# Output phase of a hybrid decoder layer: sums on VectorE over two blocks, norm weights applied in two steps

## The chip, the cores and the metric

The kernel runs on one core of a Trainium2 chip. A core has a matmul engine (TensorE, PE), VectorE (DVE), ScalarE (ACT), GpSimd (POOL) and SyncE (SP), which here only issues transfers between the main memory and the on-chip memory SBUF. Matmul results land in PSUM, eight banks of 512 float32 numbers for each of 128 partitions. The engines run side by side, each works its own queue in order, and they wait for each other by semaphores. The metric is the time of one execution in device microseconds (us), the median over several runs.

## The reference

One layer of a decoder is computed for 2048 new tokens of a prompt and for 32 sample tokens (8 sequences of 4). The width is 1024. Only the end of the layer matters here:

```python
pc = y_c @ w_out_c                              # short-convolution branch
pr = y_r @ w_out_r                              # RWKV branch
m = sigmoid(gc) * pc + sigmoid(gr) * pr         # gated merge
x = x + m @ w_o                                 # output projection and residual
y = x * rsqrt(mean(x * x, axis=-1) + 1e-6) * final_g      # last norm, a row is one token
```

All is float32. The inputs `y_c`, `y_r` and the gates come from a long first phase (projections, a convolution and the RWKV recurrence), which the change does not touch.

## The kernel before

**Products.** Each of the three projections is done for the tokens in two sets (d = 0 and 1) of 1024 rows; the sample tokens ride with set 1. A set's projection is cut into 2 x 2 quarters and computed by Strassen's scheme (in Winograd's form) with seven products of half size instead of eight. The operands of the products are sums of quarters. The sums of the weights were computed earlier and lie in main memory; those of the moving side are made here, by `make` (line 1865). To keep float32 accuracy, each operand is split into a high part (rounded by a ScalarE copy) and a low part (the rest, by a VectorE subtraction), and a product takes three matmuls: high by high, high by low, low by high.

**Stages.** `STAGES` (line 1657) orders the output phase: "r" for set 0 (RWKV branch), "o" for set 0 (output projection), "c" and "r" for set 1, "o" for set 1, seven products each, numbered through by `seq` (line 1863). Before them come some blocks of the "c" projection of set 0 (line 2062). In "c" and "r" (`merge_phase`, line 1934) the result lies with channels on the partitions. In "o" (`out_phase`, line 2001) it lies with tokens on the partitions, so that a row's norm can be taken. All products work in four blocks j of 128 partitions, and each block has its PSUM tile `acc[j]`. In "c" and "r" a block's twelve kt-by-part matmuls run one block after the other. In "o" a product takes its weights in two halves i; for each half the four blocks come in turn with six matmuls each.

**Emptying the banks.** After a block of "c" or "r", `merge_out` (line 1911) copies or adds the partial product to an SBUF quarter of M or R (called x1, x2, y1, y2), multiplies by the gate and, for "r", adds the quarter R to M (line 1930): on VectorE for x2, on POOL for the other three. After a block of "o", `out_done` (line 1964) adds the partial product to the residual rows, which were loaded into R's place. When half of a row is complete, `square` sums its squares on ScalarE. The first halves of rows (x1, y1) are complete in the products k = 1 and 4, the second halves in k = 5 and 6. Then `finish` (line 1956) adds both sums of squares, computes the reciprocal root with `rsq` (a power on POOL and a refining step in four small VectorE operations), multiplies both halves by it and by `final_g`, each with one VectorE operation over 512 columns, and stores them.

**Operands ahead.** `make(n + 2, j)` prepares the operand of the product after next into one of three rooms (UA, XH, XL) in turn, one block of 512 columns per instruction. The sums for "o" are x1 - x2 and y2 - (x1 - x2) for product k = 2 (VectorE; summed during k = 0, split during k = 1), x2 + y2 for k = 5 and y1 - y2 + (x1 - x2) for k = 6 (POOL, lines 1899, 1901, 1902).

**Samples.** Their 32 rows run as small extra matmuls (`out_samples`, line 1986) beside products of "o" in set 1: first halves in k = 0 and 1; second halves in the last product, which for this takes the weights "12" ahead of its own "22" (line 1662 orders the weights, line 2012 uses them).

**Order.** The weights stream through four buffers of 1 MB in the order of the list `order`; `take_w` issues loads up to three ahead, on SP's queue. Gates, operand quarters and residual rows go through the same queue at places fixed by `HOOKS` (line 2042). In this phase the program's text sets which operation depends on which; the order within each engine's queue is settled when the program is compiled, and ready work may come earlier than the text has it. All instructions pass through one recording helper, so the profile puts nearly all of them on line 264; tiles tell them apart.

Of the kernel before, what the change touches and what calls it, by code (L numbers as in the profile page):

```python
# [16 lines left out]
P = 128  # L17
# [327 lines left out]
def hybrid_kernel(tc, x_prompt, x_sample, state_conv, state_shift, state_rwkv, norm_g, w_in, conv_w,  # L345
# [1519 lines left out]
    def make(n, j, parts=(0, 1)):  # L1865

        if n >= len(seq):
            return
        w, d, k = seq[n]
        room = ROOMS[n % 3]  # L1870
        wd = NT if w == "o" else HW[d]
        src = Y if w != "o" else M

        def at(q):
            return src[q][:, j, 0:wd]

        def op(dst, a, b, o, eng):
            if 0 in parts:
                eng.tensor_tensor(out=dst, in0=a, in1=b, op=o)
        add, sub = ALU.add, ALU.subtract  # L1880
        if w != "o":
            t = at({0: "11", 2: "12", 3: "12", 4: "21", 5: "11", 6: "22"}.get(k, "11"))
            if k == 1:
                op(at("11"), at("12"), at("11"), sub, V)
                t = o2.tile([P, WQ], F32, name="st")[:, 0:wd]
                op(t, at("22"), at("11"), sub, V)
            if k == 2:
                op(t, at("22"), t, sub, V)
            if k == 3:
                op(t, at("22"), at("11"), sub, V)  # L1890
                op(t, at("21"), t, sub, V)
        else:
            t = at({0: "y1", 1: "x1", 3: "x1", 4: "y2", 5: "x2", 6: "y1"}.get(k, "x1"))
            if k == 2:
                op(at("x1"), at("x1"), at("x2"), sub, V)
                t = Y["21"][:, j, 0:wd]
                op(t, at("y2"), at("x1"), sub, V)
# [13 lines left out]
    def merge_out(w, d, k, j):  # L1911

        ps = acc[j][:, k == 4, 0:NT] if d == 0 else acc[j][:, :, 0:WQ // 2]

        def view(t):
            return t[:, 0:NT] if d == 0 else t.rearrange("p (a n) -> p a n", a=2)
        Q = M if w == "c" else R
        q = ("x1", "x2", "y2", "y1", "x1", "y2", "x2")[k]
        dst = view(Q[q][:, j, :])
        if k < 3:  # L1920
            A.copy(dst, ps)
            return
        g = gate_for(w, d, q, j)
        if k == 3:
            gate_mul(dst, ps, view(g))
        else:
            V.tensor_tensor(out=dst, in0=dst, in1=ps, op=ALU.add)
            gate_mul(dst, dst, view(g))
        if w == "r":
            (V if q == "x2" else G).tensor_tensor(out=M[q][:, j, 0:HW[d]], in0=M[q][:, j, 0:HW[d]], in1=R[q][:, j, 0:HW[d]], op=ALU.add)  # L1930
        if used[0] > 1:
            fetch_gate()

    def merge_phase(n):
        w, d, k = seq[n]
        room = ROOMS[n % 3]
        for j in range(NP):
# [12 lines left out]
            make(n + 2, j)  # L1950
# [4 lines left out]

    def finish(r, pieces, m=P):
        f = nwt.tile([P, 1], F32, name="fin", bufs=2)
        V.tensor_tensor(out=f, in0=fs[:, 0, r:r + 1], in1=fs[:, 1, r:r + 1], op=ALU.add)
        rsq(f, [P, 1], 1.0 / D, RMS_EPS)
        for half, (t, dst) in enumerate(pieces):  # L1960
            V.scalar_tensor_tensor(out=t, in0=t, scalar=f[0:m], in1=fg[0:m, half * 4 * P:(half + 1) * 4 * P], op0=ALU.mult, op1=ALU.mult)
            SP.store(dst, t)

    def out_done(d, k, j):
# [4 lines left out]
        if k in (1, 4, 5, 6):  # L1969
            r, half = rows_at(q, j)  # L1970
            square(o, r, half)
            if k > 4:
                finish(r, [(o_at(d, x, j), x_rows(d, x, j, y_prompt)) for x in (q[0] + "1", q[0] + "2")])
# [12 lines left out]
    def out_samples(half, base, wt, i, start, stop):  # L1986
# [6 lines left out]
    def samples_done(half):  # L1993
# [4 lines left out]
        if half:  # L1998
            finish(2 * NP, [(OS[0:NSAMP, i], y_sample.rearrange("j i d -> (j i) d")[:, i * 4 * P:(i + 1) * 4 * P]) for i in range(2)], NSAMP)

    def out_phase(n):
        w, d, k = seq[n]
        key = PRODUCTS["o"][k]
        if k == 0:
            V.memset(fs, 0.5 * D)
# [6 lines left out]
        if n == len(seq) - 1:  # L2012
            for i in range(2):
                out_samples(1, 0, take_w((w, d, "12", i)), i, i == 0, False)
            wts = [take_w((w, d, key, i)) for i in range(2)]
            for i in range(2):
                out_samples(1, NP, wts[i], i, False, i == 1)
# [6 lines left out]
        for i in range(2):  # L2024
            wt = take_w((w, d, key, i))
            for j in range(NP):
# [5 lines left out]
                if j % 2:  # L2032
                    c = 2 * i + j // 2
                    if k == 1:
                        make(n + 1, c, (1,))
                    make(n + 2, c, (0,) if k == 0 else (0, 1))
            if d and k < 2:
                out_samples(0, NP * (k == 0), wt, i, k + i == 0, k + i == 2)
        if d and k == 1:
            samples_done(0)  # L2040

# [20 lines left out]
    for i, b in enumerate(REST):  # L2062
# [13 lines left out]
        if i > 0:  # L2076
            make(0, i - 1)
    for j in range(NP):
        make(1, j)
# [35 lines left out]
```

## Time and profile before

| | |
|---|---|
| Median of three runs | 3118.93 us (3116.41 to 3121.59) |
| Profiled execution, its own time | 3117.36 us |
| Its span, first to last instruction | 3115.7 us |
| PE busy | 3017.7 us, 97% of the span |
| DVE busy | 2157.3 us, 69% |
| ACT busy | 1339.5 us, 43% |
| POOL busy | 389.5 us, 13% |
| Mean granted PE clock | 0.991 |
| Output phase, from its first matmul to the end of the span | 2648.6 to 3115.7 us |

A row of the order of time reads: start, duration, engine, operation, output from input with shapes, how many were merged into the row; in brackets how long the engine had been idle and who ended the wait. In the groups the last numbers before the bar are the total busy time and the mean of one in nanoseconds. The tile names are the kernel's, shortened: `Rx` and `Ry` are quarters of R, `Mx` and `My` of M, `acc` the PSUM tiles, `whl` the weights, `gt` the gates, `fin` and `nw` small tiles of the norm, `US` the sample operand, `OS` the sample rows.

### The profile page before, as it was taken

Reading aid. Unit: us, or ns where it says so; the run is one execution under the profiler, and the core shown is the slowest. Engines: PE = TensorE matmul, PEld = TensorE weight load, DVE = VectorE, ACT = ScalarE, POOL = GpSimd, SP = SyncE. Lnnn points to the kernel's source line nnn. Section 1 sums busy time; section 2 is a strip of 40 time slices with the busy share of each in tenths; the row PEclk is TensorE's granted clock in tenths of the full one; section 3 lists DMA queues with packets and bytes.
Section 4 is the critical chain, followed back from the end, with each engine's and each line's share of the span. In section 5 each row is a group of like instructions: output and inputs, shape, how many; then the busy total and the mean of one; then the engine's idle time right before and its main releaser. Section 6 shows DMA issues by size and latency. Waiting matters only on the chain. (4 is left out here: it accounts for less than half of the span.)

```text
span 3115.7 us, 56464 instructions
## 1 busy us (share of the span) xinstructions
PE 3017.7 (97%) x21418; PEld 2583.1 (83%) x21418; DVE 2157.3 (69%) x5713; ACT 1339.5 (43%) x2744; POOL 389.5 (13%) x568
## 2 busy tenths in 40 slices
PE   7899999999999999999999999999999999999998
PEld 6678777788778788788888889999999999779986
DVE  5577777766777777777766666766676773477675
ACT  4455555544444444444444344444444431323222
POOL 2011111111111110111111111000000000030040
PEclk9999999999999999999999999999999999999999
DMA  8687777756666676667644444444334448988765
GB/s 274 231 260 232 228 221 228 231 208 229 234 226 234 227 241 214 234 233 242 220 160 162 167 156 143 136 147 147 130 137 135 141 155 287 344 294 295 261 232 189
DMA packets 293941, 659.19 MB, mean 212 GB/s; under 512 B 46394, under 2 KB 162227, under 8 KB 242982
## 3 DMA queue, kind: packets, MB, share of 16 engines
q1 hardware_dynamic: 293670, 655.58, 62.3%
q8 instruction: 169, 2.77, 0.4%
q14 instruction: 102, 0.84, 0.1%
HBM read 472.81 MB, written 182.69 MB: 210 GB/s over the span
## 5 line engine op out<-in xcount | busy, mean ns | idle before, releaser
L264 PE MATMUL ip<-XH,whl 128*128 128x512 f32 (+3 forms) x7088 | 1944.9, 354 | 22.9 <-DVE whl L264 10.5
L264 PEld LDWEIGHTS ip<-XH,whl 128*128 128x128 f32 x7088 | 1225.9, 190 | 168.4 <-DVE whl L264 13.2
L264 PE MATMUL ip<-XL,whl 128*128 128x512 f32 (+3 forms) x3544 | 1250.4, 353 | 0.8 <-POOL XL L264 0.8
L264 PEld LDWEIGHTS ip<-XL,whl 128*128 128x128 f32 x3544 | 672.9, 190 | 71.5 <-issue 5.6
L264 DVE TENSOR_TENSOR tt<-Mi,X 128x60 f32<-128x60 f32 (+24 forms) x992 | 214.8, 217 | 28.9
L264 DVE TENSOR_TENSOR X<-X,tt 128x60 f32<-128x60 f32 (+24 forms) x992 | 211.7, 213 | 32.1
L264 DVE SCALAR_TENSOR_TENSOR S<-pb,pe,sp 64x64 f32<-64x64 f32 x512 | 143.3, 280 | 123.9 <-PE pb L264 116.9
L264 ACT ACTIVATE sp<-S,pe 128x128 f32<-128x128 f32 x256 | 102.5, 401 | 240.8 <-DVE S L264 237.5
L264 ACT COPY SV<-pb 64x128 f32<-64x128 f32 x256 | 66.1, 258 | 314.4 <-PE pb L264 312.0
L264 ACT ACTIVATE tmp<-ip,vec 128x512 f32<-128x512 f32 (+2 forms) x174 | 102.9, 593 | 206.8 <-PE ip L264 202.3
L264 DVE TENSOR_TENSOR UB<-pa,P 64x64 f32<-64x64 f32 x512 | 110.2, 215 | 117.3 <-PE pa L264 99.9
L264 DVE TENSOR_TENSOR whl<-wraw,whl 128x1024 fp32r<-128x1024 f32 x81 | 102.3, 1264 | 24.8 <-ACT whl L264 24.0
L264 ACT COPY Xbd<-Mi 32x256 f32<-32x256 f32 x128 | 88.2, 689 | 68.4 <-DVE Mi L264 66.1
L264 PEld LDWEIGHTS pb<-UB,Xbd 128*128 128x128 f32 x512 | 86.5, 189 | 33.9 <-PE ip L264 11.7
L264 ACT ACTIVATE tmp<-ip 128x512 f32<-128x512 f32 (+2 forms) x126 | 63.0, 500 | 117.9 <-PE ip L264 117.5
L264 DVE TENSOR_TENSOR GM<-pt,mask_p 128x512 f32<-128x512 f32 x128 | 82.6, 686 | 43.7 <-PE pt L264 43.4
L264 PEld LDWEIGHTS pa<-S,AR 128*128 128x128 f32 x512 | 88.9, 189 | 27.3 <-DVE S L264 14.9
L264 POOL COPY carry<-tmp 128x1 f32<-128x1 f32 x99 | 22.3, 225 | 708.2 <-ACT tmp L264 708.2
L264 PE MATMUL pb<-UB,Xbd 128*128 128x128 f32 x512 | 104.3, 285 | 3.9 <-DVE UB L264 3.1
L264 PEld LDWEIGHTS pb<-SV,BKt 128*128 128x128 f32 x512 | 89.8, 189 | 20.4 <-ACT SV L264 6.1
L264 PE MATMUL pa<-S,AR 128*128 128x128 f32 x512 | 102.1, 281 | 4.7 <-DVE S L264 4.5
L264 PE MATMUL pb<-SV,BKt 128*128 128x128 f32 x512 | 100.7, 278 | 1.4 <-ACT SV L264 1.4
(550 smaller groups left out, 4517.6 us busy)
## 6 DMA issues: line engine op xcount, KB each, us to landing
wraw<-in_w_in_dram SPq DMA_DIRECT2D x81, 512.0 KB
whl<-w_k SPq DMA_DIRECT2D x24, 1024.0 KB
whl<-w_r SPq DMA_DIRECT2D x24, 1024.0 KB
whl<-w_v SPq DMA_DIRECT2D x24, 1024.0 KB
whl<-w_z SPq DMA_DIRECT2D x24, 1024.0 KB
whl<-w_xin SPq DMA_DIRECT2D x24, 1024.0 KB
whl<-w_cg SPq DMA_DIRECT2D x24, 1024.0 KB
whl<-w_zc SPq DMA_DIRECT2D x24, 1024.0 KB
```

The source lines that it names most:

```text
L264: r = f(*a, **k)
```

## The change

All sums of the output phase go to VectorE: the additions of R to M, and the operands of the output products k = 5 and 6. `make` works on two blocks at a time, so its sums, copies and splits cover 2 x 512 columns (2 x 528 in set 1). The first half of a row is multiplied by `final_g` as soon as it is complete (`half_done`); `finish` then scales it by the row's factor with one ScalarE operation, and the second half as before with one VectorE operation. The sum of squares is scaled on the way, and the refining step gets shorter: its factor of -1/2 is put into `final_g` once. The samples' "12" weights and matmuls move from the last product to the end of product k = 1.

```diff
-            for k in ("12", "22") if (w, d, n) == ("o", 1, 6) else (k,):
+            for k in ("11", "12") if (w, d, n) == ("o", 1, 1) else (k,):
...
-    def make(n, j, parts=(0, 1)):
+    def make(n, c, parts=(0, 1)):
...
+        src, js = Y if w != "o" else M, slice(2 * c, 2 * c + 2)
+        hi, lo = (ROOMS[n % 3][:, i, js, 0:wd] for i in range(2))
...
             if k == 5:
-                op(t, t, at("y2"), add, G)
+                op(t, t, at("y2"), add)
             if k == 6:
-                op(t, t, at("y2"), sub, G)
-                op(t, t, at("x1"), add, G)
-        if 1 not in parts:
-            return
-        A.copy(room[:, 0, j, 0:wd], t)
-        V.tensor_tensor(out=room[:, 1, j, 0:wd], in0=t, in1=room[:, 0, j, 0:wd].bitcast(F32), op=sub)
+                op(t, t, at("y2"), sub)
+                op(t, t, at("x1"), add)
+        if 1 in parts:
+            A.copy(hi, t)
+            V.tensor_tensor(out=lo, in0=t, in1=hi.bitcast(F32), op=sub)
...
         if w == "r":
-            (V if q == "x2" else G).tensor_tensor(out=M[q][:, j, 0:HW[d]], in0=M[q][:, j, 0:HW[d]], in1=R[q][:, j, 0:HW[d]], op=ALU.add)
+            V.tensor_tensor(out=M[q][:, j, 0:HW[d]], in0=M[q][:, j, 0:HW[d]], in1=R[q][:, j, 0:HW[d]], op=ALU.add)
...
-            make(n + 2, j)
+            if j % 2:
+                make(n + 2, j // 2)
...
+    def half_done(t, r, m=P):
+
+        V.tensor_scalar(out=fs[0:m, 0, r:r + 1], in0=fs[0:m, 0, r:r + 1], scalar1=1.0 / D, scalar2=RMS_EPS, op0=ALU.mult, op1=ALU.add)
+        V.tensor_tensor(out=t, in0=t, in1=fg[0:m, 0:4 * P], op=ALU.mult)
+
     def finish(r, pieces, m=P):
-        f = nwt.tile([P, 1], F32, name="fin", bufs=2)
-        V.tensor_tensor(out=f, in0=fs[:, 0, r:r + 1], in1=fs[:, 1, r:r + 1], op=ALU.add)
-        rsq(f, [P, 1], 1.0 / D, RMS_EPS)
-        for half, (t, dst) in enumerate(pieces):
-            V.scalar_tensor_tensor(out=t, in0=t, scalar=f[0:m], in1=fg[0:m, half * 4 * P:(half + 1) * 4 * P], op0=ALU.mult, op1=ALU.mult)
-            SP.store(dst, t)
+
+        ms, f, z = (nwt.tile([P, 1], F32, name=f"f{i}", bufs=2)[0:m] for i in range(3))
+        V.scalar_tensor_tensor(out=ms, in0=fs[0:m, 1, r:r + 1], scalar=1.0 / D, in1=fs[0:m, 0, r:r + 1], op0=ALU.mult, op1=ALU.add)
+        G.tensor_tensor(out=f, in0=ms, in1=mhalf[0:m], op=ALU.pow)
+        V.scalar_tensor_tensor(out=z, in0=f, scalar=ms, in1=f, op0=ALU.mult, op1=ALU.mult)
+        V.scalar_tensor_tensor(out=f, in0=z, scalar=3.0, in1=f, op0=ALU.subtract, op1=ALU.mult)
+        (t0, d0), (t1, d1) = pieces
+        A.activation(out=t0, in_=t0, func=AF.Copy, scale=f)
+        V.scalar_tensor_tensor(out=t1, in0=t1, scalar=f, in1=fg[0:m, 4 * P:8 * P], op0=ALU.mult, op1=ALU.mult)
+        SP.store(d1, t1)
+        SP.store(d0, t0)
...
-                if j % 2:
-                    c = 2 * i + j // 2
+                if j == 3:
                     if k == 1:
-                        make(n + 1, c, (1,))
-                    make(n + 2, c, (0,) if k == 0 else (0, 1))
+                        make(n + 1, i, (1,))
+                    make(n + 2, i, (0,) if k == 0 else (0, 1))
...
         if d and k == 1:
             samples_done(0)
+            for i in range(2):
+                out_samples(1, 0, take_w((w, d, "12", i)), i, i == 0)
...
+    V.tensor_scalar(out=fg, in0=fg, scalar1=-0.5, scalar2=None, op0=ALU.mult)
```

More of the change, by code (lines that the diff above doesn't have):

```diff
@@ L1971, in out_done @@
             square(o, r, half)
-            if k > 4:
+            if half == 0:
+                half_done(o, r)
+            else:
                 finish(r, [(o_at(d, x, j), x_rows(d, x, j, y_prompt)) for x in (q[0] + "1", q[0] + "2")])
@@ L1984, in out_mm, with out_samples @@
                          start=start and kt + x == 0, stop=kt == NP - 1 and x == 2, skip_group_check=not start)
-    def out_samples(half, base, wt, i, start, stop):
+    def out_samples(half, base, wt, i, start):
         for kk in range(2):
@@ L1997, in samples_done @@
         square(o, 2 * NP, half, NSAMP)
-        if half:
+        if half == 0:
+            half_done(o, 2 * NP, NSAMP)
+        else:
             finish(2 * NP, [(OS[0:NSAMP, i], y_sample.rearrange("j i d -> (j i) d")[:, i * 4 * P:(i + 1) * 4 * P]) for i in range(2)], NSAMP)
@@ L2003, in out_phase @@
         key = PRODUCTS["o"][k]
-        if k == 0:
-            V.memset(fs, 0.5 * D)
         if k == 0 and d:
@@ L2075, in hybrid_kernel @@
             nc.sync.dma_start(out=fg, in_=final_g.partition_broadcast(P))
[L2076 to L2079, printed above, removed]
+        if i in (1, 3):
+            make(0, i // 2)
+    for c in range(2):
+        make(1, c)
+    V.tensor_scalar(out=fg, in0=fg, scalar1=-0.5, scalar2=None, op0=ALU.mult)
     for n, (w, d, k) in enumerate(seq):
```

34 lines of the change are left out of this document (15 added, 19 removed).

## The prediction

> **What bounds the kernel now.** I read the page first, then the busy time by window, then the order of time around every place where the matmul engine (PE) stood still.
>
> ```profile
> span 3115.7 us, 56464 instructions
> ...
> PE 3017.7 (97%) x21418; PEld 2583.1 (83%) x21418; DVE 2157.3 (69%) x5713; ACT 1339.5 (43%) x2744; POOL 389.5 (13%) x568
> ```
>
> PE is busy for 97% of the span. The edit can only return what PE loses, so I cut the second half of the output phase at the starts and ends of its products (columns: busy microseconds and instruction count of each engine, granted PE clock, DMA share, GB/s).
>
> ```profile
> core 0: us, PE busy (x) PEld busy (x) DVE busy (x) ACT busy (x) POOL busy (x), PEclk, DMA share, GB/s
> 2722.30:2744.55 22.25, 22.25 (x97) 18.03 (x96) 17.33 (x24) 4.95 (x8) 12.64 (x9) 1.00 0.86 296
> 2743.70:2775.99 32.29, 25.50 (x102) 19.52 (x100) 32.12 (x33) 5.91 (x11) 20.14 (x13) 0.89 0.73 271
> 2744.55:2809.47 64.92, 58.13 (x242) 45.95 (x240) 49.57 (x60) 14.71 (x28) 19.29 (x13) 0.95 0.78 291
> 2755.67:2775.99 20.32, 13.53 (x50) 9.83 (x48) 20.25 (x21) 4.56 (x8) 12.11 (x8) 0.83 0.61 222
> 2787.21:2798.34 11.13, 11.13 (x49) 9.01 (x48) 5.36 (x9) 3.69 (x8) 0.00 (x0) 1.00 0.79 286
> 3007.28:3029.81 22.53, 15.29 (x58) 10.81 (x57) 22.43 (x26) 5.01 (x9) 12.71 (x8) 0.92 0.52 185
> 3029.81:3042.80 12.99, 12.99 (x58) 10.10 (x57) 6.37 (x11) 4.29 (x10) 0.00 (x0) 1.00 0.48 161
> 3087.41:3103.63 16.22, 15.18 (x65) 10.95 (x63) 14.82 (x49) 3.73 (x11) 3.25 (x5) 1.00 0.60 202
> 3103.63:3115.70 12.07, 0.00 (x1) 0.00 (x0) 7.75 (x27) 1.11 (x4) 1.64 (x3) 0.63 0.46 174
> ```
>
> An undisturbed output product of 48 matmuls takes 11.13 us (2787.21 to 2798.34); one with eight sample matmuls on top takes 12.99. Against these, four places lose time. The first output product (y1, right after the "r" products of set 0) takes 20.32 instead of 11.13: 9.19 lost. The same product of set 1 takes 22.53 instead of 12.99: 9.54 lost. The last product takes 16.22 for 48+16 matmuls. And after the last matmul 12.07 us pass until the span ends. In both slow products VectorE (DVE) is busy without a break (20.25 of 20.32, 22.43 of 22.53), and POOL is busy for 12 us of each. The order of time in the first one:
>
> ```profile
> 2743.30 1.63 POOL L264 TENSOR_TENSOR My<-My,My 128x512 f32<-128x512 f32 x1
> ...
> 2755.54 1.40 DVE L264 TENSOR_TENSOR Y<-My,Mx 128x512 f32<-128x512 f32 x1
> ...
> 2756.34 1.75 POOL L264 TENSOR_TENSOR My<-My,Mx 128x512 f32<-128x512 f32 x1
> 2756.86 1.78 DVE L264 SCALAR_TENSOR_TENSOR Rx<-gt,Rx 128x512 f32<-128x512 f32 x1
> ...
> 2760.01 0.68 DVE L264 TENSOR_TENSOR Rx<-Rx,acc 128x512 f32<-128x512 f32 x1
> ...
> 2760.75 1.88 PE L264 MATMUL acc<-whl,XH 128*128 128x512 f32 x6 [2.14 <-DVE Rx L264]
> ...
> 2765.54 8.71 PE L264 MATMUL acc<-whl,XH 128*128 128x512 f32 x30 [2.91 <-DVE Rx L264]
> ...
> 2775.99 0.70 PE L264 MATMUL acc<-whl,XL 128*128 128x512 f32 x2 [1.74 <-ACT XH L264]
> ```
>
> PE waits 2.14 and 2.91 us for Rx<-Rx,acc: that is DVE's sum in merge_out that takes the fourth partial product out of a PSUM bank, and the next product needs the bank. The matmuls of a block end every 2.8 us, but the sums of the third and fourth block start only behind the gate multiplications and the sums of make in DVE's queue. Those are slow: the gate multiplication at 2756.86 takes 1.78 us while POOL runs My<-My,Mx. The 1.74 us put down to ACT I read as DVE too: the product that starts there reuses the bank which Ry<-Ry,acc emptied late. So 6.79 us are waits. The rest of the 9.19, 2.40 us, is slower matmuls: granted clock 0.83 there, 1.00 in the undisturbed product. The set 1 product shows the same:
>
> ```profile
> 3012.25 1.66 PE L264 MATMUL acc<-whl,XH 128*128 128x512 f32 x6 [2.02 <-DVE Rx L264]
> 3017.07 2.17 PE L264 MATMUL acc<-whl,XH 128*128 128x512 f32 x6 [3.17 <-DVE Rx L264]
> ...
> 3028.84 1.14 PE L264 MATMUL acc<-whl,US 128*64 128x512 f32 x4 [2.06 <-DVE Ry L264]
> ```
>
> 7.25 us of waits, so 2.29 of its 9.54 are matmuls at the clock of 0.92.
>
> **What makes DVE late.** One row gives the pace of DVE alone, one the price of a double-width operation, three the price beside POOL (mean ns of one in the window 2743.7 to 2776):
>
> ```profile
> 2687.01 3.70 DVE L264 TENSOR_TENSOR Y<-Y,Y 128x512 f32<-128x512 f32 x6
> ...
> L264 DVE TENSOR_TENSOR whl<-wraw,whl x81: 1183/1224/2314, 22.8 to 628.2; 128x1024 fp32r<-128x1024 f32 x81
> ...
> L264 DVE TENSOR_TENSOR Y<-My,Mx 128x512 f32<-128x512 f32 x4 | 6.3, 1585 | 0.0
> ...
> L264 DVE SCALAR_TENSOR_TENSOR Rx<-gt,Rx 128x512 f32<-128x512 f32 x4 | 5.5, 1376 | 0.0
> ...
> L264 DVE TENSOR_TENSOR Rx<-Rx,acc 128x512 f32<-128x512 f32 x4 | 2.7, 678 | 0.0
> ```
>
> Six sums of 512 in 3.70 us are one per (3.70-0.68)/5 = 0.604 us. The same kind of instruction has means of 1585 and 1376 ns in the window where POOL adds; the sum with one operand in PSUM keeps 678. So the price falls on operations with both operands in SBUF while POOL reads SBUF. The window row 2743.70 holds 33 DVE instructions; at 0.604 they are 19.9 us, and 32.12 were used: 12.2 us is the price of POOL's 13 sums (20.14 us on POOL).
>
> **The change, part by part.** The sum is made against the profiled execution: span 3115.7, its own time 3117.36, so 1.66 lies around the span. It is 1.6 below the median of the three runs shown (3118.93).
>
> *Sums from POOL to DVE.* The 13 POOL sums of the window become 13 x 0.604 = 7.9 us of DVE work, and the 12.2 us of slowing go. Only two of the 13 (M+=R of block 3 and the one before) feed the next products; the other eleven make operands of the sixth and seventh output product, over 50 us later (five products of 11.13). That POOL ran one at 2743.30, inside the last "r" product, although line 1901 is reached only from the fifth output product, shows that engines take ready work out of the order of the text. Needed in the window: 19.9 + 1.2 = 21.1 us; the window without PE's loss is 32.29 - 9.19 = 23.1. It fits, and nothing is left to wait for. If all 13 run inside it, 27.8 us stand against 23.1: 4.7 us stay as a wait. Bounds per transition: 0 and 4.7. I take 0.5, near the lower end, because the eleven have the latest use. Moved to the later products they are covered: an undisturbed product leaves DVE idle for 11.13 - 5.36 us. In the two "r" products before the window (row 2722.30) DVE would have 24 + 9 instructions, 19.9 of 22.25 us: full, but not over. Gain: 9.19 + 9.54 - 1.0 = 17.7 us; this counts the clock as restored.
>
> *Two blocks in one instruction.* 1.224 us (median) for 1024 elements against 2 x 0.604 = 1.21: nothing saved, nothing lost. The Trainium skill (VectorE: DVE Perf Modes, "The TRN2 errata") says that each SBUF operation pays a fixed extra latency that one large tile pays once; from its formula, 151 cycles at 0.96 GHz, I estimate 0.16 us saved a pair, for the 17 such operations of the window some 1.3 us of DVE time; the trace does not agree for queued operations, whose starts already lie 0.604 apart, and the sum is the same either way as long as DVE is not the bound. The pair halves the choice points: a bank sum can now stand behind 1.22 us instead of 0.68. In the output products the fourth block's sum has three groups of six matmuls, 3 x 1.39 = 4.2 us, before PE needs its bank again (24 matmuls are half of 11.13, so six are 1.39). It is hidden until more than 4.2 us stand in front.
>
> *The "12" weights and their eight sample matmuls*, from the last product to just after the second. The matmuls cost 12.99 - 11.13 = 1.86 us in either place. In the last product a DMA wait goes:
>
> ```profile
> 3087.60 6.27 DMA whl<-uo
> ...
> 3093.92 1.15 PE L264 MATMUL acc<-whl,US 128*64 128x512 f32 x4 [1.04 <-DMA whl<-uo]
> ```
>
> The last product falls from 16.22 to 12.99, and the second rises by 1.86: net gain 1.37. On the SP queue two loads of 1 MB pass in front of eight others. Four weight buffers rotate, so the first t2 load starts when the first half of "11" is used up and is needed after the second half (5.6), its own four sample matmuls (0.9) and the eight moved ones (1.9): 8.4 us. The load above took 6.27 with output stores beside it. It fits by 2.1; bounds 0 and, if x rows in front of it double it, 12.5 - 8.4 = 4.1. I take 0, because that product moves 161 GB/s where the first set's products moved 291.
>
> *Row ends.* Of the last row block today: sum, square, five small operations, and the eight multiplications of the four row blocks in one DVE queue, the last of which ends at 3112.32. After: half the multiplications are done an output product earlier, the other half's first operand goes to ScalarE. Latencies of one block:
>
> ```profile
> 3083.43 0.69 DVE L264 TENSOR_TENSOR Ry<-Ry,acc 128x512 f32<-128x512 f32 x1 [6.27 <-PE acc L264]
> 3084.22 0.63 ACT L264 ACTIVATE junk<-Ry 128x512 bf16<-128x512 f32 x1 [6.23 <-DVE Ry L264]
> 3084.76 0.19 ACT L264 ACTIVATION_READ_ACCUMULATOR junk<-Ry 128x1 f32 x1
> ...
> 3085.61 0.15 DVE L264 TENSOR_SCALAR nw<-fin 128x1 f32<-128x1 f32 x1
> 3085.85 0.55 POOL L264 TENSOR_TENSOR fin<-nw,mhalf 128x1 f32<-128x1 f32 x1 [59.41 <-DVE nw L264]
> ...
> 3086.43 0.16 DVE L264 TENSOR_TENSOR nw<-fin 128x1 f32<-128x1 f32 x1 [0.66 <-POOL fin L264]
> ...
> 3110.72 0.16 DVE L264 TENSOR_TENSOR fin<-fin,nw 128x1 f32<-128x1 f32 x1
> 3110.91 0.75 DVE L264 SCALAR_TENSOR_TENSOR Ry<-Ry,fin,fg 128x512 f32<-128x512 f32 x1
> 3111.58 0.74 DVE L264 SCALAR_TENSOR_TENSOR Rx<-Rx,fin,fg 128x512 f32<-128x512 f32 x1
> ...
> 3112.35 0.33 SPq L337 DMA_DIRECT2D out_dram<-Rx  x1
> ```
>
> From the bank sum (taken as the end of PE) to the square 0.79, to the end of the accumulator read 1.52, to the mean 1.57 (0.05 taken over); mean to power 0.24, power to the next DVE operation 0.58, between the two small ones and to the multiplication 0.19 each: 2.77. Multiplication to store issue 0.77, last issue to the end of the span 3115.70 - 3112.35 = 3.35: together 6.9. A second store behind it adds 0.4 (0.33 issue): 7.3. The third block's multiplication (0.75) falls at the time of the fourth block's sum; I add 0.3: 7.6. Gain 12.07 - 7.6 = 4.5. Bounds 6.9 and 9.0 (another two multiplications in the way). ScalarE's multiplication is not in the trace in this form; its squares of 512 take 0.63, shorter than DVE's 0.75, and it runs beside that. It waits for DVE's last small operation, and behind it on ScalarE stands the next block's square, which isn't due for another 2.8 us.
>
> *The early multiplications*: 17 times 0.68 + 0.15 us, and -0.5 times fg once, between 0 and the 1.22 of the double-width row; I take 1. In the product that gets four of them DVE is busy for 6.37 of 12.99, so 3.3 more are hidden; they would cost at most 4 x 0.83 if DVE were full. The memsets of fs go. The scaling of fg waits for fg's load; behind it in DVE's queue are sums for the second "r" product, which PE reaches 11 us later. The first "r" product, where the same operations come in pairs, I take as unchanged.
>
> **Sum.** 17.7 + 1.4 + 4.5 = 23.6; 3117.4 - 23.6 = 3093.8, so 3094. Own range: 3090 (no residue, a row end of 6.9, and the 2.5 by which the lowest run lies under the median) to 3102.
>
> **The rivals.**
> - *DVE takes POOL's place as the bound.* All 13 sums run in each window: 4.7 instead of 0.5, twice, 3102. For it: DVE had no idle time there. Against it: late use. Chance 0.17.
> - *The clock stays low.* The 2.40 + 2.29 come from elsewhere than from the waits: 3098.5. For it: the clock is a grant, not a wait. Against it: the product right behind has 1.00. The Trainium skill (TensorE: Matmul & The Clock Gate, "What's actually happening") ties the low clock to an idle window of about 3.4 us; by that rule the single waits here, 3.17 at most, would cost no clock, and the trace, with 0.83, does not agree. Chance 0.08.
> - *DMA becomes the bound after the first transition.* From 2744.55 to 2809.47 291 GB/s x 64.92 us = 18.9 MB were moved; in 55.7 us that is 339. If 291 were all, the 9.19 stay lost: 3103. Against it: 0.78 share, so 291/0.78 = 373 can be had. Chance 0.07.
> - *The order, not POOL, makes the sums late.* DVE would still put five operations a block ahead of the next bank sum; only the last product and the row end gain: 3117.4 - 5.9 = 3111.5. For it: five operations at 0.604 are 3.0 us for a block, PE needs 2.8. Against it: 0.2 a block is not 9. Chance 0.10.
> - *Slower: pairs in front of the bank sums.* Place: the three output products of each set whose operands need sums (t2, t1, 22). If both pairs, with four double sums (4.9), two copies on ScalarE that must wait for PE to leave the operand (twice a square's 0.63 each, 2.5) and two low parts (2.4), plus the bank sum (0.7), come before PE's bank is free, that is 10.5 against 4.2: 6.3 lost in each of six products, 38 us, 3132. It decides from 4.2 us of queue on. For it: DVE works its queue in order, and a low part cannot start before its copy. Against it: the copies and low parts of four blocks stand there today without a wait of PE, in a product with 5.36 us of DVE work. Chance 0.06.
>
> **How the numbers follow.** Forecast 0.52, rivals as above. The range takes in all but the last two rivals and reaches part of the way to 3111.5: 3089 to 3109. What three runs can tell from no change is about 0.2%, 6.2 us: slower is the last rival, 0.06; half of the 3111.5 case and nothing else is within, 0.05; faster 0.89.
>
> **What would show it.** Right: no DVE operation of 512 above 0.8 us in the windows of the transitions, the first output product of each set near 11.2 and 13.0 us at a clock of 1.00, the second product of set 1 near 14.9, no DMA wait in the last one, 7 to 8 us after the last matmul. Wrong: PE waits for DVE of more than 2 us in those products, POOL idle and DVE still without a gap, waits for whl behind the second product, or a row end above 9.

## The result and the profile after

The changed kernel takes 3098.56 us (median of four runs, 3096.35 to 3100.6) against 3117.67 us for the kernel before (four runs, 3115.36 to 3121.59): a ratio of 0.9937, 95% interval 0.992 to 0.9955. In a second series of runs it took 3096.2 us (five runs, 3092.32 to 3103.68) against 3116.88: 0.9935, interval 0.9921 to 0.9949. It is faster, by about 0.6%, and the forecast of 3094.0 us is 4.6 and 2.2 us below the two medians.

The page of the kernel after:

```profile
span 3098.7 us, 56080 instructions
...
PE 3014.9 (97%) x21418; PEld 2582.2 (83%) x21418; DVE 2142.9 (69%) x5606; ACT 1337.9 (43%) x2691; POOL 318.3 (10%) x520
```

PE has the same 21418 matmuls and hardly less busy time; what went is idle time. Busy time by window, columns as in the prediction. The first row is the last "r" product of set 0, the next three are the first three output products of set 0; then come the first three output products of set 1, the last product, the row end, the transition of set 0 as a whole, and the whole output phase:

```profile
core 0: us, PE busy (x) PEld busy (x) DVE busy (x) ACT busy (x) POOL busy (x), PEclk, DMA share, GB/s
2748.99:2760.14 11.15, 11.15 (x50) 9.02 (x49) 10.97 (x16) 1.05 (x1) 0.00 (x0) 1.00 0.98 361
2760.14:2771.29 11.15, 11.15 (x49) 9.00 (x48) 10.56 (x14) 2.82 (x3) 0.00 (x0) 1.00 0.97 367
2771.29:2782.42 11.13, 11.13 (x50) 9.01 (x49) 10.85 (x13) 3.78 (x7) 0.00 (x0) 1.00 0.91 340
2782.42:2793.55 11.13, 11.13 (x49) 9.01 (x48) 7.01 (x12) 3.37 (x7) 0.00 (x0) 1.00 0.87 331
3002.08:3015.06 12.98, 12.98 (x58) 10.09 (x57) 12.69 (x16) 4.20 (x5) 0.00 (x0) 1.00 0.59 204
3015.06:3029.89 14.83, 14.83 (x65) 11.17 (x64) 12.04 (x19) 4.93 (x11) 0.00 (x0) 1.00 0.45 150
3029.89:3041.03 11.14, 11.14 (x50) 8.97 (x48) 5.78 (x9) 1.81 (x4) 0.00 (x0) 1.00 0.91 366
3074.41:3088.46 14.05, 13.39 (x57) 9.89 (x55) 11.10 (x32) 8.12 (x18) 3.78 (x6) 1.00 0.53 196
3088.46:3098.70 10.24, 0.00 (x1) 0.00 (x0) 3.21 (x10) 2.36 (x6) 1.10 (x2) 0.65 0.41 154
2748.00:2780.30 32.30, 32.30 (x140) 26.12 (x140) 31.50 (x40) 7.59 (x9) 0.00 (x0) 1.00 0.95 353
2654.15:3098.70 444.55, 433.65 (x2504) 379.94 (x2504) 290.23 (x408) 130.12 (x195) 12.52 (x17) 0.99 0.78 283
```

The first output products take 11.15 and 12.98 us (before 20.32 and 22.53), at a clock of 1.00, with POOL idle and DVE still almost full (10.56 of 11.15, 12.69 of 12.98). The waits of PE from 2655 us, just behind the first matmul of this phase, to the end, and two of the groups of DVE in the transition:

```profile
engine line waited for: us in total, times, longest us
PE acc L264 <- DVE OS L264: 0.7, 1, 0.7
```

```profile
line engine op names shapes xcount | busy us, mean ns | idle before us <-releasers
L264 DVE SCALAR_TENSOR_TENSOR Rx<-gt,Rx 128x512 f32<-128x512 f32 x4 | 2.7, 684 | 0.0
L264 DVE TENSOR_TENSOR Y<-My,Mx 128x1024 f32<-128x1024 f32 x2 | 2.4, 1219 | 0.0
```

One wait is left, in the last product. The gate multiplication has a mean of 684 ns (before 1376), and the sum for t2 costs 1219 ns for two blocks (before 1585 for one). So a full DVE was no bound in itself; before, the same engine was full because its instructions were slow.

The output phase, from its first matmul to the end of the span, fell from 467.09 us (2648.61 to 3115.7) to 444.55: 22.5 us, where 23.6 were forecast. The own time of the profiled execution fell less, from 3117.36 to 3100.6, or 16.8 us, because this phase began at 2654.15 and not at 2648.61. No line of the first phase differs between the two kernels. More on that at the end; it is why the experiments are compared by the length of the output phase, beside the times.

### The profile page after: what moved, and what is told of

It is laid out like the page before. It is cut to its first block, busy times and chain, and to the rows that moved or that the text cites. A ratio compares the mean times of both kernels' runs of the same rounds, so it can differ in the third digit from the quotient of the medians.

```text
span 3098.7 us, 56080 instructions
## 1 busy us (share of the span) xinstructions
PE 3014.9 (97%) x21418; PEld 2582.2 (83%) x21418; DVE 2142.9 (69%) x5606; ACT 1337.9 (43%) x2691; POOL 318.3 (10%) x520
## 5 line engine op out<-in xcount | busy, mean ns | idle before, releaser
L264 PE MATMUL acc<-XL,whl 128*128 128x264 f32 (+1 forms) x616 | 97.9, 309 | 0.0
```

The costliest lines, as they stand in the source:

```text
L264: r = f(*a, **k)
```

## The experiments

In each the output phase is measured from its first matmul to the end of the span, "row end" from the end of the last matmul. The reference lengths are those of the two profiles of the kernel after, 444.55 and 444.99 us, and of the two of the kernel before, 467.09 and 466.78.

**1. The kernel before once more.** No edit.

> The kernel before, unchanged, for a second profile: which of its lengths repeat. If the untouched first phase only varies from execution to execution, the output phase (first acc matmul to the end of the span) is again 467.1 us within 0.6, the first output products are again near 20.3 and 22.5 us, the last product near 16.2 and 12.1 us follow the last matmul, while the start of the output phase may lie anywhere from 2645 to 2655. The first r product (12.31 in the first profile) is between 11.1 and 12.4: a value near 11.2 means that the 1.2 us gained there after the change are no gain of the change.

Output phase 466.78 us; first output products 20.30 and 22.54; row end 11.81; first "r" product 12.15. These lengths repeat within 0.3 us. The phase began at 2648.72.

**2. The kernel after once more**, timed.

> The changed kernel once more, beside the next three on the same chip. If the first phase, which is the same instructions in all kernels, starts the output phase at a time that varies from execution to execution (2645.5 to 2654.2 us in six profiles so far), the output phase repeats at 444 to 445 us while the total moves by several us; the median should then lie near 3095, between 3091 and 3099. If the changed kernel itself delays its first phase, the output phase begins at 2654 again.

3096.2 us; output phase 444.99, first output products 11.16 and 12.98, row end 10.28, first "r" product 11.50. The lengths repeat within 0.5 us, but the phase began at 2649.31 instead of 2654.15. So about 5 us of the first profile's time were not the change's.

**3. Only the sums, in single blocks.** The kernel before with its four kinds of POOL sums on VectorE:

```diff
-                op(t, t, at("y2"), add, G)
+                op(t, t, at("y2"), add, V)
...
-                op(t, t, at("y2"), sub, G)
-                op(t, t, at("x1"), add, G)
+                op(t, t, at("y2"), sub, V)
+                op(t, t, at("x1"), add, V)
...
-            (V if q == "x2" else G).tensor_tensor(out=M[q][:, j, 0:HW[d]], ...
+            V.tensor_tensor(out=M[q][:, j, 0:HW[d]], ...
```

> The kernel before with one part of the change alone: all POOL sums (R added to M, operands of output products k = 5 and 6) go to VectorE, one block per instruction as before. Theory A (POOL's reads slow VectorE, and that makes the bank sums late): the first output products fall from 20.3 and 22.5 us to 11.2 to 12 and 13.0 to 14, no VectorE operation of 512 there above 0.8 us; the last product and the row end stay at 16.2 and 12.1. Time 3099 (3117.7 - 18.7), between 3097 and 3103. Theory B (the order in VectorE's queue makes them late, and two blocks per instruction cure it): both products stay above 17 us, time 3112 to 3118.

3101.0 us, ratio 0.9934 (0.9912 to 0.9956); output phase 447.32; first output products 11.15 and 12.97; row end 12.13. The window of the first one of set 0:

```profile
2754.70:2765.85 11.15, 11.15 (x50) 9.02 (x48) 10.91 (x18) 4.15 (x7) 0.00 (x0) 1.00 0.92 348
```

This alone returns 19.6 of the 22.2 us (466.9 - 447.3, of 466.9 - 444.8, means of the two profiles). With single blocks PE waits as little as with pairs: the pairs bring nothing in these products, and cost nothing.

**4. The kernel after with those sums back on POOL**, pairs kept:

```diff
-                op(t, t, at("y2"), add)
+                op(t, t, at("y2"), add, G)
...
-            V.tensor_tensor(out=M[q][:, j, 0:HW[d]], ...
+            (V if q == "x2" else G).tensor_tensor(out=M[q][:, j, 0:HW[d]], ...
```

(and the same for the two sums of k = 6).

> The changed kernel with one part undone: the sums that were on POOL are on POOL again, with two blocks per instruction where make issues them. Theory A: both first output products are again above 17 and 19 us, with VectorE operations of 1.2 to 2.4 us beside POOL; only the last product and the row end keep what they gained in the changed kernel (2.2 and 1.8 us). Time about 3098.6 + 18.7 = 3117, between 3110 and 3118. Theory B: products near 11.2 and 13.0, time 3098 to 3101.

3114.42 us (ten runs), ratio 0.9986 (0.9976 to 0.9996); output phase 463.91; first output products 20.34 and 21.88. The time is lost again. The first product of set 0, the same with the 12 us ahead of it, and groups of DVE in the longer window:

```profile
2751.76:2772.10 20.34, 13.14 (x49) 9.94 (x48) 20.17 (x15) 4.08 (x4) 11.41 (x4) 0.90 0.66 245
2739.76:2772.10 32.34, 25.14 (x101) 19.65 (x100) 32.03 (x25) 5.68 (x6) 18.73 (x8) 0.94 0.77 281
```

```profile
L264 DVE TENSOR_TENSOR Y<-My,Mx 128x1024 f32<-128x1024 f32 x2 | 6.5, 3250 | 0.1
L264 DVE SCALAR_TENSOR_TENSOR Rx<-gt,Rx 128x512 f32<-128x512 f32 x4 | 5.5, 1374 | 0.1
```

DVE runs 25 instructions in 32.34 us here, 40 in 32.30 in the kernel after, and is full in both.

**5. Idle reads on POOL.** The kernel after, with multiplications of an unused tile on POOL after each sum of R into M, 24 in a set, over 528 columns. They read SBUF and nothing uses their result; a ScalarE copy of one column makes each wait for its block. DVE's instructions and their order are those of the kernel after (all 5606 of them, in the traces):

```diff
+            A.copy(dum[:, 0:1], R[q][:, j, 0:1])
+            for _ in range(3 if q == "x2" else 1):
+                G.tensor_tensor(out=dum[:, 0:WQ], in0=dum[:, 0:WQ], in1=dum2.broadcast_to([P, WQ]), op=ALU.mult)
```

> The changed kernel plus idle work on POOL whose result nobody uses: for each block of the r products k = 3 to 6, ScalarE copies one column of the fresh block into a spare tile, and POOL then multiplies 528 columns of that tile in place (once a block, three times in k = 6), 24 per set as many as the sums that left POOL. VectorE's instructions and their order are the same as in the changed kernel. Theory A: VectorE's operations with both operands in SBUF take 1.2 to 1.8 us beside POOL's, the two first output products become 14 to 20 and 16 to 22 us, time 3106 to 3118. Theory B: products stay at 11.2 and 13.0, time 3098 to 3101.

3114.87 us (ten runs), ratio 0.9986 (0.9976 to 0.9997); output phase 462.77; first output products 19.89 and 21.30. The same window, and groups of DVE and POOL:

```profile
2758.01:2777.90 19.89, 13.13 (x49) 9.91 (x48) 19.89 (x16) 2.57 (x5) 16.66 (x11) 0.91 0.72 256
```

```profile
L264 DVE SCALAR_TENSOR_TENSOR Rx<-gt,Rx 128x512 f32<-128x512 f32 x4 | 5.3, 1333 | 0.0
L264 DVE TENSOR_TENSOR Rx<-Rx,acc 128x512 f32<-128x512 f32 x4 | 2.7, 675 | 0.0
...
L264 POOL TENSOR_TENSOR dum<-dum,dum 128x528 f32<-128x528 f32 x14 | 20.9, 1491 | 9.6 <-ACT dum L264 8.9
```

No sum waits for POOL here and DVE's order is unchanged, and yet the whole loss is back. So it is something that POOL does while it works that slows DVE, not who makes the sums or in which order. The sum with one operand in PSUM keeps 675 ns.

**6. Idle writes on POOL.** As before, but each multiplication replaced by two memsets of 704 columns: POOL is about as busy and reads nothing:

```diff
-                G.tensor_tensor(out=dum[:, 0:WQ], in0=dum[:, 0:WQ], in1=dum2.broadcast_to([P, WQ]), op=ALU.mult)
+                G.memset(dum, 0.0); G.memset(dum, 0.0)
```

> As the run with idle POOL multiplications, but POOL writes constants over 704 columns (two fills for each multiplication, about 0.65 us each) and reads nothing. Theory A in the form that POOL's reads count: VectorE keeps 0.68 and 1.22 us, products 11.2 and 13.0, time 3098 to 3101. If any work on POOL slows VectorE (writes, or its waits): as with the multiplications, above 3105. The Trainium skill (SBUF - State Buffer, Who interferes with whom) says that a VectorE instruction with two SBUF inputs contends with a GpSimd instruction that reads SBUF, not with one that only writes it; this run tests that sentence here.

3090.42 us, ratio 0.9905 (0.9885 to 0.9925); output phase 444.00; first output products 11.15 and 12.98:

```profile
2752.17:2763.32 11.15, 11.15 (x49) 9.01 (x48) 10.56 (x14) 3.39 (x6) 9.68 (x15) 1.00 0.98 366
```

```profile
L264 DVE SCALAR_TENSOR_TENSOR Rx<-gt,Rx 128x512 f32<-128x512 f32 x4 | 2.7, 684 | 0.0
...
L264 POOL MEMSET dum<- 128x704 f32 x24 | 16.5, 687 | 8.2 <-ACT dum L264 7.2
```

POOL is busy for 9.68 of 11.15 us, and DVE's multiplication keeps 684 ns. The ScalarE copies are there as in experiment 5, and DVE's order is the same; what is gone is POOL's reads and the arithmetic on what was read. So it is POOL's reads of SBUF, as far as the two can be told apart. The Trainium skill (SBUF — State Buffer, "Who interferes with whom") states just this: a DVE instruction with two SBUF inputs contends with a GpSimd instruction that reads SBUF, not with one that only writes. The traces agree, also for the operation with one operand in PSUM. Its output phase is that of the kernel after within 1 us, so the lower time of this kernel is not explained by this phase; it began at 2646.20.

**7. The norm alone.** The kernel before with the new `half_done` and `finish` and -1/2 in `final_g`; sums on POOL, "12" in the last product. (The edit consists of the lines that the change has in these functions.)

> The kernel before with the new norm alone (first half multiplied early, ScalarE's scaling, shorter refining step); sums on POOL, the 12 weights in the last product. Theory N, the norm's new form makes the row end shorter: 10.2 us after the last matmul (before 12.07), last product as before, output phase 467.1 - 1.9 = 465.2. Theory W, it is the samples' move that frees VectorE in the last blocks: 11.5 to 12.1 us after the last matmul, output phase 466.5 to 467.1. Both: first output products 20.3 and 22.5 as before; if the early multiplications (0.83 us each) are not covered beside POOL, up to 3.3 us more in the product that has them.

Own time of the one run 3115.17; output phase 465.03, 1.9 less than the mean before; row end 10.04 (before 12.07 and 11.81). So the new norm makes the row end shorter, as theory N had it, by 1.9 and not by 4.5. The first output product of set 1 and the one behind it:

```profile
3005.67:3028.65 22.98, 15.30 (x59) 10.79 (x57) 22.88 (x27) 4.81 (x9) 12.80 (x8) 0.91 0.50 182
3028.65:3042.84 14.19, 14.19 (x57) 10.99 (x56) 7.15 (x15) 4.28 (x10) 0.00 (x0) 0.91 0.39 148
```

The second, which has the early multiplications, takes 14.19 us instead of 12.99. PE waits for nothing in it and DVE is busy for 7.15 us: the early multiplications are covered, and the 1.2 us are the clock of 0.91. It follows a longer wait at the end of the product ahead (PE's waits in that one; 2.06 in the kernel before):

```profile
PE acc L264 <- DVE Rx L264: 4.0, 2, 2.1
PE acc L264 <- DVE Ry L264: 3.6, 1, 3.6
```

**8. The "12" weights alone.** The kernel before with the order of loads and `out_samples` moved:

```diff
-            for k in ("12", "22") if (w, d, n) == ("o", 1, 6) else (k,):
+            for k in ("11", "12") if (w, d, n) == ("o", 1, 1) else (k,):
...
-            for i in range(2):
-                out_samples(1, 0, take_w((w, d, "12", i)), i, i == 0, False)
...
             samples_done(0)
+            for i in range(2):
+                out_samples(1, 0, take_w((w, d, "12", i)), i, i == 0, False)
```

> The kernel before with the move of the 12 weights and their eight sample matmuls alone; sums on POOL, norm in the old form. Both theories: second output product of set 1 near 14.85 us instead of 12.99, no wait for a transfer in the last product, whose matmuls and wait for the samples' sum take 14.0 to 14.4 instead of 16.22. Theory N: 12.0 us after the last matmul as before, output phase 466.6 to 467.1. Theory W: near 10.2 after the last matmul, output phase 465.0.

Own time of the one run 3119.4; output phase 466.65, 0.3 less than the mean before. The second product of set 1 and the matmuls of the last one:

```profile
3031.84:3047.49 15.65, 15.65 (x65) 11.80 (x64) 7.45 (x13) 5.17 (x12) 0.00 (x0) 0.94 0.42 143
```

```profile
3092.10 2.00 PE L264 MATMUL acc<-whl,US 128*64 128x512 f32 x8
3093.93 11.28 PE L264 MATMUL acc<-whl,XH 128*128 128x512 f32 x48
```

The last product has no wait at all and takes 13.11 us (3092.10 to 3105.21), 3.1 less. But the second one takes 15.65, 0.8 of it by a clock of 0.94, the row end 12.49, and the first output product 23.26. Alone, the move is worth nothing that shows.

The three parts alone give 19.6 + 1.9 + 0.3 = 21.8 us; together 22.2. They add up: the 0.4 between them, which is all that is left for the pairs, is no more than the lengths differ from run to run.

**9. The last bank sum ahead of the previous rows.** In the kernel after, the row end is longer than forecast. Its last two blocks in order of time:

```profile
3079.85 8.61 PE L264 MATMUL acc<-whl,XH 128*128 128x512 f32 x36 [0.66 <-DVE OS L264]
...
3087.15 0.68 DVE L264 TENSOR_TENSOR Rx<-Rx,acc 128x512 f32<-128x512 f32 x1
...
3088.68 0.16 DVE L264 SCALAR_TENSOR_TENSOR f<-fs 128x1 f32<-128x1 f32 x1 [0.19 <-ACT junk L264]
3088.92 0.55 POOL L264 TENSOR_TENSOR f<-f,mhalf 128x1 f32<-128x1 f32 x1 [2.14 <-DVE f L264]
3089.50 0.41 DVE L264 SCALAR_TENSOR_TENSOR f<-f,f 128x1 f32<-128x1 f32 x2 [0.66 <-POOL f L264]
...
3089.95 0.75 DVE L264 SCALAR_TENSOR_TENSOR Rx<-Rx,f,fg 128x512 f32<-128x512 f32 x1
3090.62 0.68 DVE L264 TENSOR_TENSOR Rx<-Rx,acc 128x512 f32<-128x512 f32 x1
...
3094.59 0.38 SPq L337 DMA_DIRECT2D out_dram<-Rx  x1
```

PE ends at 3079.85 + 8.61 = 3088.46, and the sum of its last block starts only at 3090.62, 2.16 us later: in DVE's queue the whole chain of the block before stands ahead of it, with a wait of 0.66 for POOL's power inside. From sum to sum it is 3.47 us (3087.15 to 3090.62), where PE delivers a block every 2.8. The edit makes the refining step of block j wait, in DVE's order, for the bank sum of block j+1:

```diff
-        V.scalar_tensor_tensor(out=z, in0=f, scalar=ms, in1=f, ...
+        r_ = V.scalar_tensor_tensor(out=z, in0=f, scalar=ms, in1=f, ...
+        if after:
+            tc.add_manual_dep(r_.ins, after.ins.name, ...)
...
-                out_done(d, k, j)
+                bank = out_done(d, k, j, True)
+                if j:
+                    last_rows(d, j - 1, bank)
+            last_rows(d, NP - 1)
```

> The changed kernel with the last product's order in VectorE's queue changed: the bank sum of block j+1 stands ahead of the last two small operations and the multiplication of block j, which wait for POOL's power. Theory T1 (the row end is 10 us because each bank sum stands behind the previous block's chain of about 3.4 us, against PE's 2.8 a block): bank sums follow their matmuls by 0.1 us, after the last matmul 7.4 us instead of 9.7 to 10.2. Theory T2 (the stores set the end): still 9.7 or more.

```profile
3089.60 0.69 DVE L264 TENSOR_TENSOR Rx<-Rx,acc 128x512 f32<-128x512 f32 x1 [0.91 <-PE acc L264]
3090.21 0.41 DVE L264 SCALAR_TENSOR_TENSOR f<-f,f 128x1 f32<-128x1 f32 x2
...
3092.14 0.41 DVE L264 SCALAR_TENSOR_TENSOR f<-f,f 128x1 f32<-128x1 f32 x2 [0.66 <-POOL f L264]
```

The last sum now waits for PE (0.91) and not for the queue. The row end is 8.33 us (after 10.24 and 10.28; 7.4 was expected), the output phase 443.23, 1.5 less. In experiments 4 to 6, which end with the same code as the kernel after, the row end is 9.70 to 9.77, so the order is worth 1.4 to 1.9. The time, 3097.27 us (3093.27 to 3099.73), ratio 0.9931 (0.9917 to 0.9944), doesn't tell it from the kernel after.

**10. Another PSUM tile for the samples.** The 0.66 us that PE waits in the last product are for the samples' sum, because block 1 comes to the tile that also holds the samples. The edit puts the second halves into block 3's tile:

```diff
-                T.matmul(acc[half][0:2 * NSAMP, 1, :], ...
+                T.matmul(acc[3 * half][0:2 * NSAMP, 1, :], ...
...
-            V.tensor_tensor(out=o, in0=o, in1=acc[half][i * NSAMP: ...
+            V.tensor_tensor(out=o, in0=o, in1=acc[3 * half][i * NSAMP: ...
```

> The changed kernel with the second halves of the sample rows accumulated in the PSUM tile of block 3 instead of block 1. Theory S1 (the last product has a wait of 0.66 us and slower matmuls behind it because block 1 waits until VectorE has read the samples out of its tile): the wait goes, the last product with its eight sample matmuls falls from 14.05 to 13.0. Theory S2 (the wait is for VectorE being late in general): it appears ahead of another block, 14.0.

The wait for OS is gone and another has come, because block 3's tile is emptied last in the product before:

```profile
3076.19 2.06 PE L264 MATMUL acc<-whl,US 128*64 128x512 f32 x8 [0.32 <-DVE Ry L264]
3078.09 10.13 PE L264 MATMUL acc<-whl,XH 128*128 128x512 f32 x43
```

The last product takes 13.66 us instead of 14.05, and the row end 10.88 instead of 10.24: PE ends earlier and the rows don't. Output phase 445.33, time 3096.52 (3095.26 to 3100.98), ratio 0.9938 (0.9925 to 0.995): no gain. While DVE's chain sets the pace of the last blocks, PE's wait in the same product costs nothing.

**11. Both.**

> Both of the last two edits together. If T1 and S1 hold, the output phase falls from 444.3 to about 441 us (2.3 + 1.0 less), and the median lies 3 us under the changed kernel's; if neither holds, no difference.

Output phase 442.04 us, 2.7 less than the kernel after; last product 13.66, row end 7.98. The time is 3094.01 us (3087.76 to 3097.1), ratio 0.9923 (0.9909 to 0.9936), the lowest of the four that were timed together (the kernel after and experiments 9 to 11), though its interval overlaps that of the kernel after. With the chain out of the way, the tile's wait counts, and the two edits bring more (2.7) than their single values together (1.5 and -0.6).

## Why the prediction was right, and where it was off

**The total.** The output phase fell by 22.5 us where 23.6 were forecast, and part of this closeness is luck. The sums gave 1.0 more than forecast, and the first "r" product, which was taken as unchanged, another 1.2; the row ends gave 2.7 less and the "12" weights 1.0 less. The measured 3098.56 us is also the time that the rival of a lasting low clock gave (3098.5), but the clock is 1.00 in both transitions, so it is not that rival that came true. Of the signs of being wrong, two are there: a row end above 9 us, which marks the step that failed, and a DVE without a gap beside an idle POOL. The second was a bad sign to choose, since PE waits for nothing there.

**Sums from POOL to DVE: right in mechanism and size.** Forecast 17.7 us; measured in the two products 20.32 - 11.15 and 22.53 - 12.98, together 18.7. The cause was put on POOL's reads beside DVE instructions with both operands in SBUF, and experiments 5 and 6 show it. The residue of 0.5 each did not come. The later sums went into the next two products, as argued: DVE is busy for 10.56, 10.85 and 7.01 us in the first, second and third output product of set 0, with no wait of PE.

**The clock: right.** It is 1.00 in both products after, and 0.90 and 0.91 in experiments 4 and 5, where the waits are back. That it follows the waits is shown by this coming and going, not how. The 0.83 of the slow product before is a mean: in windows within it the clock is 1.00 up to 2760.75 us, through the first wait, 0.50 between 2763.00 and 2768.00, and 1.00 again from 2771.00.

**Two blocks: right for the time, off in its working.** Experiment 3 and the kernel after have the same product times. But the prediction set the duration of a double operation (1.224) against the distance of starts of two single ones (2 x 0.604). Two queued double sums of the kernel after show their distance, 2.35 - 1.22 = 1.13 us:

```profile
2776.20 2.35 DVE L264 TENSOR_TENSOR My<-My,Mx 128x1024 f32<-128x1024 f32 x2
```

So 1.21 - 1.13 = 0.08 us is saved a pair. The 17 operations that the prediction counted are single ones, eight pairs, and save some 0.7 us of DVE time; with POOL's former sums the transition has 16 double operations, some 1.3 us. The Trainium skill (VectorE: DVE Perf Modes, "The TRN2 errata") has the direction right, against what the prediction said of it; its 0.16, as estimated there, is twice the size. PE gains nothing by it here.

**The "12" weights: off.** The second product rose by 1.84, as forecast, and no load is waited for. The last product takes 14.05 instead of 12.99 us. The step that failed is that nothing but the DMA wait stood in it: the samples' sum on DVE came 0.66 late, behind the row chains of the product before. Alone (experiment 8) the move does give 13.11. The other 0.4 of the 1.06 is not traced.

**Row ends: the step that failed.** 4.5 us forecast, 1.8 measured (12.07 to 10.24); 10.24 lies outside the bounds of 6.9 and 9.0. The prediction took the last bank sum as coming at the end of PE, with 0.3 for the third block's multiplication. It comes 2.16 later, since DVE's queue holds the third block's chain, with its wait for POOL, ahead of it; that is 1.86 of the 2.64 that are missing, and experiment 9 gets 1.4 to 1.9 back by the order alone. Another 0.76 is the time from the last store issue to the end of the span: 4.11 (3094.59 to 3098.70) where 3.35 was taken from the kernel before. There the last two stores are issued 0.66 apart, here 0.42. In all 13 profiles the time is 3.08 to 3.35 where they are 0.66 apart (four profiles) and 3.56 to 4.15 where they are 0.42 to 0.45 apart (nine); whether the distance is why was not separated. The latencies of the chain itself were right: from the last sum to the first store issue it is 3094.17 - 3090.62 = 3.55, forecast 0.79 + 0.73 + 0.05 + 0.24 + 0.58 + 0.38 + 0.77 = 3.54.

**Not in the sum: the first "r" product**, 12.31 and 12.15 us before and 11.12 and 11.50 after. It is also 11.15 and 11.14 in experiments 7 and 8, where the sums stay on POOL. So it isn't the sums. The traces show a wait in it: PE waits 0.90 us for DVE's `My` in the first profile before (0.74 in the second), 0.32 in experiment 9, and not at all in the two profiles after or in experiments 7 and 8:

```profile
2676.64 1.78 PE L264 MATMUL acc<-UA,whl 128*128 128x512 f32 x7
2679.33 9.79 PE L264 MATMUL acc<-UA,whl 128*128 128x512 f32 x41 [0.90 <-DVE My L264]
```

`My` is a gate multiplication that empties a bank. In DVE's queue it stands behind a sum that waits 2.65 us for a transfer of `Y`; this sum starts 0.14 us behind the product's first matmul in the first profile before, and 1.93 ahead of it in experiment 7. So this gain hangs on when a transfer lands; why it lands earlier was not separated.

**Not in the sum: the first phase.** The forecast was made against one execution's own time. In the 13 profiles the output phase begins between 2645.49 us (experiment 4) and 2654.67 (experiment 9), for a first phase whose lines are the same in all. Within one kernel, the kernel after, it is 2654.15 and 2649.31. The spread of 9.2 us is larger than all that was forecast beside the transitions (1.4 + 4.5), and larger than the 4.6 by which the forecast missed.

**The rivals.** DVE as the bound: it is full and PE doesn't wait. The clock: see above. DMA as the bound: 353 GB/s at a share of 0.95 over the transition, 367 in its fastest product, more than the 339 that were asked for, without a wait of PE. The order and not POOL: experiment 5 keeps the order and has the loss. Slower by pairs in front of the bank sums: the products whose operands are made in pairs take 11.12 to 11.15 us. In the last blocks, though, something of this kind did happen, on a small scale: a chain in front of a bank sum cost 2.16 us, not in PE's time but behind it.

## What to carry to other kernels

An operation on POOL that reads SBUF can double the time of DVE's operations with both operands in SBUF (here 684 to 1333 ns), so work moved off a full DVE can make it fuller; look at the mean of one operation beside POOL and without it before counting busy shares. At the end of a kernel look in the order of the last engine's queue for waits of an earlier block that stand in front of the last result. And when a change is worth less than the spread of a phase that it doesn't touch, measure it by the length of the phase that it does.

## What the runs showed of the hardware beside this

- The first phase varies by 9.2 us between the 13 profiles, all with the same lines in it. In the windows between 100 and 120 us from the start the clock was granted differently in the kernel before and in the kernel after:

```profile
100.00:120.00 20.00, 19.31 (x93) 14.55 (x93) 12.66 (x28) 11.21 (x20) 1.40 (x6) 0.92 0.78 262
```

```profile
100.00:120.00 20.00, 20.00 (x73) 15.02 (x72) 7.72 (x10) 8.63 (x17) 0.92 (x5) 0.62 0.69 228
```

  With 0.62 PE issued 73 matmuls, with 0.92 it issued 93. The clock is 0.60 to 0.71 there in five of the 13 profiles (the first one after, experiments 5, 8, 9 and 10) and 0.91 to 1.00 in the others; experiment 8 is the kernel before with nothing but its weights moved, so this does not come with the new sums. The kernel after falls 4.6 us behind the kernel before between its 300th and its 500th matmul (73.1 and 123.3 us before, 73.9 and 128.7 after), and the other four lose 4.4 to 4.6 in the same place. That isn't the whole of it: in experiment 11 the clock is 0.91 there and the output phase still begins at 2653.16. Why the clock is granted so stays open.
- The lower clock behind a wait can fall into the next product. In experiments 7 and 8 the product behind the slow one has no wait and a clock of 0.91 and 0.94, in the kernel before 1.00; in experiment 7 it is 0.60 in the first 3.35 us of this product and 1.00 behind them; the last wait ahead of it was 3.6 us in both experiments and 2.06 before. The Trainium skill (TensorE: Matmul & The Clock Gate, "What's actually happening") ties the low clock to an idle window of about 3.4 us. The 3.6 agree with it; the kernel before, which lost clock within the slow products with single waits of 3.17 us at most, does not.
- DMA moved 367 GB/s at a share of 0.97 while PE, DVE and ScalarE were at work, without a wait of PE.
